# Gated-delta scans: the decayed state on ScalarE, finer convolution budgets, the attention's preparation in 27 parts and its loads in another order

## The chip, the cores and the metric

The kernel runs on one core of a Trainium2 chip. The metric is device time in microseconds (us) of one execution. Engines are named as in the profile: PE is TensorE (matmuls), PEld its weight loads, DVE VectorE, ACT ScalarE, POOL GpSimd, SP the engine that here issues the DMAs. One engine runs its instructions strictly in the order of its own queue, so an instruction that waits holds up all that stands behind it on that engine.

## The reference, cut to what matters

One layer of a hybrid backbone: 512 latent and 256 context tokens of width 2048 go through one input projection; 8 heads of a bidirectional gated delta network (GDN) and 8 heads of attention (2 key/value heads) read it; the joined result, gated by SiLU, goes through one output projection.

```python
def step(s, inp):                       # one chunk of 64 tokens of one head, one direction
    q_i, k_i, u_i, w_i, g_i, intra_i = inp
    v_new = u_i - w_i @ s
    o_i = (q_i * exp(g_i)) @ s + intra_i @ v_new
    s = s * exp(g_last) + (k_i * exp(g_last - g_i)).T @ v_new
    return s, o_i
...
qkv_g = silu(centred_conv(qkv_g, conv_w))              # 5 taps, per channel
qa, ka = apply_rope(rms_norm(qa), cos, sin), apply_rope(rms_norm(ka), cos, sin)
attn_lat = block_attention(qa, k_all, v_all) * silu(z_a)
y = concatenate([gdn_lat, attn_lat]) @ w_out
```

The line of interest is the state's: the old state `s` is scaled by one number per direction and head, and a product is added.

## The kernel before, in words

**Stages.** Modulation and the first projections fill the first 160 us of the span; eight scans, one per GDN head, run to about 860 us; the attention to about 1085; the output projection to about 1240; then a tail. Nearly every projection is made of three 512-column matmuls for each pair of 128x128 blocks (a weight is split into a high part `whi` and a low rest `wlo`). Such a weight piece takes a DMA into `wraw`, a cast to `whi` on ScalarE (L130) and a subtraction to `wlo` on VectorE (L131), with three buffers each.

**A scan.** `gdn_scan(h)` runs 12 chunk steps of head h, both directions side by side (`st` is 128x2x128). A step is a chain over three engines: PE multiplies the state by keys and queries into `ks` (L937, L939 or L942); VectorE makes `r` (L951, two halves; `rh` in the profile); PE makes `ts` from it (L956); ScalarE scales it to `vs` (L960, `vsh`); PE multiplies by `ktok` (L972); VectorE adds the decayed state `sd` and writes the new state (L978, `sth`). `sd` is the old state times its decay. It is one POOL multiply (recorded at L289, the line of the helper `mul`; `sdh` in the profile) that needs the old state, has one buffer, and is needed only by L978.

**What fills the waits of the chain.** Each of the three parts of a step yields a number of matmul columns, `F1, F2, F3 = 3900, 2700, 3200`. The driver loop pulls that many columns of projection matmuls from `feeding()` (L185) into PE's queue, so that PE works while the chain is on other engines. The parts are counted by a slot number: slot%3 = 0 stands ahead of L956, 1 ahead of L972, 2 ahead of the next `ks`. Into the same slots go the preparation of the next head (`gdn_prep(h+1)`, one part at each slot named in `PREP_AT`, with its cost in us), and the convolution jobs: the projections' results wait in a list of jobs, five taps each, the first on ScalarE and four on VectorE (L248, about 0.75 us each), then a tanh on ScalarE and products on VectorE (L286). `step_jobs` draws jobs in order while a budget is left: `CAP = (1.0, 1.6, 1.9)` by slot%3, less `spent[0]`, which holds the slot's preparation cost and 0.7 for each weight piece loaded in it.

**The last head.** Head 7 has no next head to prepare. Its slots carry `attn_prep()` instead, at the slots in `LATE_AT`: for two key/value heads and the first query head, a transpose on PE of what was stored by the projections (`kvch`, read back by DMA), squares and their sum on ScalarE (L1023), a factor by VectorE and POOL's power (L1024, L283), the product (L1026, `ktok`), the rotary table (loaded by DMA, multiplied by the norm weight; `IB` in the profile, whose room it uses), the rotation, transposes and high/low splits. V goes through the same transposes (`vtp`, L1041).

**The attention.** Units u = 0 to 16 each take one half of the queries of one head (u = 2h + qp); PE transposes the probabilities (`pt`, L1391), ScalarE and VectorE copy and split them (`pth` L1036, `ptl` L1037). ACT, DVE and POOL run in the order written there. `fill(n)` draws n pieces of three matmuls of the gate projection (`zl`, L1462), `fill(n, 2)` also two rows of the output gate (`gacc`, L1510). SP loads the merge inputs before the units: eight `o_d[i]` into `M[i]`, then `zad[i]` into `M[8+i]`, which unit u = i reads (L1567). The sixteen `M` are split into `mh` and `ml` for the output projection by `merged` (L1600).

**Before the first scan** the same `pull` lets PE run projections while the gate decays (`gates`, `gcp` L596) and the first `gdn_prep` are made.

What sets the order of instructions on an engine in the scans is a scheduler by priority, and `first_of_all()` (2500) puts `sd`, `r`, `vs` and the state update ahead of what is ready beside them; in the attention it is the written order.

Of the kernel before, what the change touches and what calls it, by code (L numbers as in the profile page):

```python
# [69 lines left out]
def build(tc, a):  # L70
# [940 lines left out]
    def rope_table(tb, i):  # L1011

        SY.dma_start(tb.rearrange("p s t d -> p (s t d)"), a["rope"])
        wv = A["nw"][:, i:i + 1]
        mul(V, tb[:, 0], tb[:, 0], wv.to_broadcast([128, 4, 128]))
        for t in range(4):
            x = tb[:, 1, t:t + 1].rearrange("p t (a s r) -> p (t a) s r", a=2, s=2)
            mul(V, x, x, swapped(wv))
        return tb

    def head_norm(ps, n, ss, jk, out):
        for t in range(n):
            S.activation(jk, ps[:, t], AF.Square, accum_out=ss[:, t:t + 1])  # L1023
        V.tensor_scalar(out=ss[:, :n], in0=ss[:, :n], scalar1=1.0 / 128.0, scalar2=EPS, op0=ALU.mult, op1=ALU.add)  # L1024
        power(ss[:, :n], -0.5)
        V.tensor_tensor(out=out, in0=ps, in1=ss[:, :n].unsqueeze(2).to_broadcast([128, n, 128]), op=ALU.mult)  # L1026

    def rope_apply(y, tb, t2):

        mul(V, t2.rearrange("p t (a s r) -> p (t a) s r", a=2, s=2), swapped(y),  # L1030
            tb[:, 1].rearrange("p t (a s r) -> p (t a) s r", a=2, s=2))
        mul(V, y, y, tb[:, 0])
        V.tensor_tensor(out=y, in0=y, in1=t2, op=ALU.add)
# [10 lines left out]
    def attn_prep():  # L1044
# [25 lines left out]
        def normed(tp, n, nm, tb, out):  # L1070
            ss = gp.tile([128, 10], F32, tag="ss", bufs=2, name=f"ss{nm}")
            NT = gp.tile([128, 6, 64], F32, tag="NT", bufs=1, name=f"NT{nm}")
            head_norm(tp, n, ss, NT[:, 0:2].rearrange("p a b -> p (a b)"), out)
            if tb is None:
                mul(V, out, out, nw[:, 1:2].to_broadcast([128, n, 128]))
                return
            t2 = gp.tile([128, 6, 128], F32, tag="vtok", bufs=2, name=f"rt2{nm}")
            rope_apply(out, tb, t2[:, :4])
# [4 lines left out]
        rope_table(tabk, 1)
        for kv in range(2):
            base = 6 * kv
            for t0, n in parts:
# [6 lines left out]
            for t0, n in parts:
                yield
                tp = transposes(chs, t0, n, bank(f"vtp{kv}{t0}")[:, :n])
                split_from(tp, vah[:, t0:t0 + n, kv * 128:kv * 128 + 128], val[:, t0:t0 + n, kv * 128:kv * 128 + 128])
# [626 lines left out]
```

## Time and profile before

| | |
|---|---|
| three runs | 1273.0, 1273.27, 1273.49 us; median 1273.27 |
| the profiled execution | 1274.02 us, its span 1271.9 us |
| TensorE clock granted in it | 0.993 of full speed on average |
| ScalarE, POOL busy | 570.1 us, 156.8 us |

The span is the time from the first to the last instruction that the profile holds; the execution's own time is 2.1 us longer. A wait for a named engine is the idle time of one engine just before an instruction, put down to what released it. A name like `sdh` stands for `sd` of any head, since numbers are left out.

### The profile page before, as it was taken

What the parts mean: (1) busy time and instruction counts of PE and PEld (TensorE: products, weight loads), DVE (VectorE), ACT (ScalarE), POOL (GpSimd) and SP (SyncE); (2) the same over time, 40 slices, a digit from 0 to 9 for tenths busy, and PEclk for the clock granted to TensorE, in tenths of its full rate; (3) what the DMA queues carried; (4) which work ended last, traced back from release to release, by engine and by line L of the source; (5) the groups of instructions that cost most, each with busy time, mean ns of one, the idle gap of its engine ahead of it and who ended that gap; (6) DMA issues with size and microseconds to landing.
All of it is one profiled execution on the core that took longest, in us unless ns stands there. A gap on an engine that the chain in (4) does not pass through costs nothing.

```text
span 1271.9 us, 24265 instructions
## 1 busy us (share of the span) xinstructions
PE 1235.5 (97%) x9242; PEld 1016.2 (80%) x9242; DVE 853.9 (67%) x1905; ACT 570.1 (45%) x1452; POOL 156.8 (12%) x206
## 2 busy tenths in 40 slices
PE   6899999999999999999999999999999999999997
PEld 4566788888888888888888887877888888787886
DVE  5444597596876778677786655547998997555433
ACT  5222373445545454454545444545555443434211
POOL 1222100111111111121211112200000000000000
PEclk9899999999999999999999999999999999999999
DMA  9999524132332223322233444357454443565202
GB/s 354 318 332 346 155 75 109 48 72 61 76 72 78 60 64 67 78 65 64 68 64 78 101 112 146 101 161 240 137 153 125 136 130 100 183 225 193 96 33 99
DMA packets 227287, 164.52 MB, mean 129 GB/s; under 512 B 62243, under 2 KB 198524, under 8 KB 226148
## 3 DMA queue, kind: packets, MB, share of 16 engines
q1 hardware_dynamic: 226874, 162.87, 44.1%
q8 instruction: 73, 1.20, 0.4%
q14 instruction: 43, 0.34, 0.1%
q10 hardware_dynamic: 297, 0.11, 0.0%
HBM read 148.85 MB, written 14.08 MB: 128 GB/s over the span
## 4 chain that ended last, share of the span: by engine, by line
PE 79%; DVE 10%; DMA 4%; ACT 3%; issue 3%; SPq 0%; POOL 0%; ACTq 0%; POOLq 0%; DVEq 0%
PE zl L1462 9%; PE kl L185 5%; PE ql L185 4%; PE vl L185 4%; PE po L148 3%; PE po L147 3%; PE po L149 3%; PE kvl L185 3%; PE tsh L972 3%; PE kx L185 2%; PE ada L404 2%; PE vx L185 2%; PE tsh L956 2%; PE klat L471 2%; PE pt L1391 2%
## 5 line engine op out<-in xcount | busy, mean ns | idle before, releaser
L960 ACT ACTIVATE vsh<-tsh,cch 128x128 f32<-128x128 f32 x88 | 32.4, 368 | 226.7 <-PE tsh L956 226.7
L289 POOL TENSOR_TENSOR sdh<-sth,egl 128x256 f32<-128x256 f32 x80 | 70.7, 884 | 445.2 <-DVE sth L978 364.3
L951 DVE SCALAR_TENSOR_TENSOR rh<-ksh,negeg,vtokh 64x128 f32<-64x128 f32 x176 | 61.2, 347 | 24.1 <-PE ksh L939 18.0
L148 PE MATMUL po<-wlo_wo,mh 128*128 128x512 f32 x192 | 76.1, 396 | 0.2 <-DVE wlo_wo L131 0.2
L147 PE MATMUL po<-whi_wo,mh 128*128 128x512 f32 x192 | 76.1, 397 | 0.0
L149 PE MATMUL po<-whi_wo,ml 128*128 128x512 f32 x192 | 76.0, 396 | 0.0
L1462 PE MATMUL zl<-hhL,whi_z 128*128 128x512 f32 x176 | 71.4, 405 | 0.0
L1462 PE MATMUL zl<-hL,whi_z 128*128 128x512 f32 x176 | 69.7, 396 | 0.0
L1462 PE MATMUL zl<-hhL,wlo_z 128*128 128x512 f32 x176 | 69.4, 395 | 0.0
L131 DVE TENSOR_TENSOR wlo_wo<-wraw_wo,whi_wo 128x512 fp32r<-128x512 f32 x48 | 33.0, 689 | 51.2 <-ACT whi_wo L130 51.1
L978 DVE TENSOR_TENSOR sth<-sdh,tsh 128x256 f32<-128x256 f32 x80 | 33.7, 421 | 44.0 <-PE tsh L972 35.7
L130 ACT CAST whi_wo<-wraw_wo 128x512 fp32r<-128x512 f32 x48 | 29.7, 618 | 57.8 <-PE po L149 47.5
L972 PE MATMUL tsh<-vsh,ktok 128*128 128x128 f32 x352 | 54.3, 277 | 0.4 <-ACT vsh L960 0.4
L972 PEld LDWEIGHTS tsh<-vsh,ktok 128*128 128x128 f32 x352 | 48.0, 191 | 3.5 <-ACT vsh L960 0.6
L1036 ACT CAST pth<-pt 128x512 fp32r<-128x512 f32 x48 | 26.5, 586 | 44.3 <-PE pt L1391 44.3
L185 PE MATMUL vl<-hhL,whi_v 128*128 128x512 f32 x112 | 46.3, 413 | 0.0
L967 ACT ACTIVATE oqh<-ksh,egsw 64x128 f32<-64x128 f32 x128 | 45.9, 358 | 0.8
L185 PE MATMUL vl<-hhL,wlo_v 128*128 128x512 f32 x112 | 46.2, 413 | 0.0
L185 PE MATMUL vl<-hL,whi_v 128*128 128x512 f32 x112 | 45.6, 408 | 0.0
L1510 DVE SCALAR_TENSOR_TENSOR gacc<-graw,scol,gacc 128x512 f32<-128x512 f32 x60 | 44.9, 748 | 1.1
L147 PEld LDWEIGHTS po<-whi_wo,mh 128*128 128x128 f32 x192 | 36.1, 188 | 9.6 <-ACT ze L1416 0.8
L148 PEld LDWEIGHTS po<-wlo_wo,mh 128*128 128x128 f32 x192 | 36.1, 188 | 9.2 <-DVE wlo_wo L131 0.6
(545 smaller groups left out, 3901.0 us busy)
## 6 DMA issues: line engine op xcount, KB each, us to landing
wada<-in_w_ada SPq DMA_DIRECT2D x64, 512.0 KB, 8.6
graw<-in_w_ada SPq DMA_DIRECT2D x64, 256.0 KB, 3.0
wraw_wo<-in_w_out SPq DMA_DIRECT2D x48, 256.0 KB, 3.0
wraw_z<-in_w_in SPq DMA_DIRECT2D x44, 256.0 KB, 3.0
wraw_v<-in_w_in SPq DMA_DIRECT2D x28, 256.0 KB, 3.1
wraw_k<-in_w_in SPq DMA_DIRECT2D x24, 256.0 KB, 2.9
wraw_q<-in_w_in SPq DMA_DIRECT2D x24, 256.0 KB, 2.8
xs<-in_x SPq DMA_DIRECT2D x4, 1024.0 KB, 8.4
```

Of the source, the lines that this page charges most:

```text
L131: (lo_eng or G).tensor_tensor(out=lo, in0=raw, in1=hi, op=ALU.subtract)
L147: T.matmul(out, lhsT=lh, rhs=rh, start=start, stop=False, skip_group_check=True)
L148: T.matmul(out, lhsT=lh, rhs=rl, start=False, stop=False, skip_group_check=True)
L149: T.matmul(out, lhsT=ll, rhs=rh, start=False, stop=stop, skip_group_check=True)
L185: T.matmul(out, lhsT=lw, rhs=rt[m], start=k == 0 and n == 0, stop=k == KT - 1 and n == 2, skip_group_check=True)
L289: eng.tensor_tensor(out=out, in0=x, in1=y, op=ALU.mult)
L951: behind["DVE"] = V.scalar_tensor_tensor(out=r[rows], in0=ks[rows, d], scalar=gsc["negeg"][rows, gcol:gcol + 1], in1=vtok[rows, p], op0=AL ...
L967: S.activation(oq[rows, v, p - 2], ks[rows, d], AF.Copy, scale=gsc["egsw"][rows, gcol:gcol + 1])
L972: T.matmul(ts[:, d], lhsT=ktok[:, p, half], rhs=vs, start=True, stop=True, skip_group_check=True)
L978: behind["DVE"] = V.tensor_tensor(out=sn, in0=sd, in1=ts[:, 0:2], op=ALU.add)
L1462: T.matmul(pl, lhsT=lw, rhs=rt, start=k == 0 and m == 0, stop=k == KT - 1 and m == 2, skip_group_check=True)
L1510: V.scalar_tensor_tensor(out=acc, in0=raw, scalar=scol[:, k:k + 1], in1=acc, op0=ALU.mult, op1=ALU.add)
```

## The change

**The decayed state.** POOL's one multiply becomes two ScalarE copies with a scale read per partition, one for each direction, at the same place in the code.

**The budgets.** A VectorE job is drawn while more than 0.2 us of budget is left, not more than 0. Five costs in `PREP_AT` rise: 1.3 to 1.6 at slots 16, 17, 19 and 20, and 0.9 to 1.1 at slot 21.

**The attention's preparation.** Its 15 parts, which stood at the odd slots 1 to 27 and at 33, are cut into 27, at slots 0, 4 to 14, 16 to 29 and 31. The helpers are cut apart: loading the rotary table, its cosine and sine products, squares, scaling, and two halves of the rotation are parts or pieces of parts of their own. The tables and `kvch` are loaded a few slots ahead of their use.

**Ahead of the scans**, one pull grows from 22000 to 25500 columns, and the first of the pulls around `gdn_prep(0)` shrinks from 5000 to 2500.

**The attention.** `M[8+i]` is loaded just before `M[i]`, for each i below NZA, so `M[8]` comes first and `M[12]` in ninth place. In the last unit `fill(3)` stands before the third `pt`. `merged(0)`, the first split for the output projection, moves from the head of the output projection into unit 12.

```diff
-        while jobs and (kind is None or kind == jobs[0][0]) and (budget > 0 if jobs[0][0] == "D" else act):
+        while jobs and (kind is None or kind == jobs[0][0]) and (budget > 0.2 if jobs[0][0] == "D" else act):
...
                         sd = gp2.tile([128, 2, 128], F32, tag="sd", bufs=1, name=f"sd{nm}_{si}")
-                        eg = egl[:, :, gcol:gcol + 1]
-                        mul(G, sd, st, (eg if dt_ == 0 else eg[:, ::-1]).to_broadcast([128, 2, 128]))
+                        for d in range(2):
+                            S.activation(sd[:, d], st[:, d], AF.Copy, scale=egl[:, d ^ dt_, gcol:gcol + 1])
...
         kn = ktoks[0].rearrange("p a s d -> p (a s) d")
+        rope_load(tabk)
         chs = load(kvd[0], "kvch00", NTOK)
-        rope_table(tabk, 1)
+        yield
+
         for kv in range(2):
...
+            tp0 = transposes(chs, 0, 2, bank(f"kps{kv}0")[:, :2])
+            r0 = squares(tp0, 2, f"k{kv}0")
+            yield
+            tp1 = transposes(chs, 2, 4, bank(f"kps{kv}2"))
+            r1 = squares(tp1, 4, f"k{kv}2")
+            chs = load(kvd[2 + kv], f"kvch{kv}1", NTOK)
+            if kv == 0:
+                yield
+                rope_cos(tabk, 1)
+                yield
+                rope_sin(tabk, 1)
+            yield
+            scaled(y0, tp0, r0)
+            mul(V, y0, y0, nw[:, 1:2].to_broadcast([128, 2, 128]))
+            yield
+            scaled(y1, tp1, r1)
+            t2 = rope_one(y1, tabk, f"k{kv}")
             if kv == 1:
-                rope_table(A["tab"], 0)
+                rope_load(A["tab"])
+            yield
+            tp = transposes(chs, 0, 2, bank(f"vtp{kv}0")[:, :2])
+            split_from(tp, vah[:, 0:2, vsl], val[:, 0:2, vsl])
+            yield
+            rope_two(y1, tabk, t2)
+            yield
...
-               18: 0, 19: 1.3, 20: 1.3, 21: 0.9, 26: 0.6, 27: 0.6, 29: 1.2, 31: 0.3, 33: 1.5}
-    LATE_AT = dict.fromkeys((*range(1, 28, 2), 33), 1.5)
+               18: 0, 19: 1.6, 20: 1.6, 21: 1.1, 26: 0.6, 27: 0.6, 29: 1.2, 31: 0.3, 33: 1.5}
+    LATE_AT = dict.fromkeys((0, *range(4, 15), *range(16, 30), 31), 1.5)
...
-    pull(22000)
+    pull(25500)
...
-    for n in (5000, 5500, 0, 0, 5500, 0, 4000, 0, 0, 14000, 0, 0, 0, 0, 0):
+    for n in (2500, 5500, 0, 0, 5500, 0, 4000, 0, 0, 14000, 0, 0, 0, 0, 0):
...
     for i in range(8):
+        if i < NZA:
+            SY.dma_start(M[8 + i], zad[i])
         SY.dma_start(M[i], o_d[i])
-    for i in range(NZA):
-        SY.dma_start(M[8 + i], zad[i])
...
+        if h >= NH:
+            fill(3)
         if before is not None:
             pts.append(attn_pt(before[0], before[1], before[2], 2))
...
+        if u == 2 * NH - 4:
+            merged(0)
...
-            if first:
+            if first and k:
                 merged(k)
```

VectorE in head 5 between the state update of step 7 and `r` of step 8 (`sth_7`, `rh_8`; `tmh` and `NEh` belong to the next head's preparation, `cacc_q` is a convolution tap, `kq` and `kc` the products at a convolution's end). Before:

```order
L832 TENSOR_TENSOR tmh_7589<-NEh_7578 96x14
L834 TENSOR_TENSOR NEh_7578<-NEh_7578,tmh_7589 96x14
L978 TENSOR_TENSOR sth_7_7832<-sdh_7_7782,tsh_7_7803 128x256
L131 TENSOR_TENSOR wlo_kv_0_7840<-wraw_kv_0_7837,whi_kv_0_7839 128x512
L248 SCALAR_TENSOR_TENSOR cacc_q_7777<-craw_1554,cvT,cacc_q_7777 128x512 x2
L951 SCALAR_TENSOR_TENSOR rh_8_7851<-ksh_7293,negeg,vtokh_6645 64x128 x2
```

After:

```order
L978 TENSOR_TENSOR sth_7_7884<-sdh_7_7836,tsh_7_7858 128x256
L131 TENSOR_TENSOR wlo_kv_0_7890<-wraw_kv_0_7887,whi_kv_0_7889 128x512
L286 SCALAR_TENSOR_TENSOR kq_7450<-craw_1553,cacc_k_7679 128x4x64
L286 SCALAR_TENSOR_TENSOR kc_7451<-craw_1553,cacc_k_7679 128x2x64
L951 SCALAR_TENSOR_TENSOR rh_8_7903<-ksh_7341,negeg,vtokh_6692 64x128 x2
```

The two taps ahead of `rh_8` have left this place, and two shorter products stand there, since taps drawn later come later in the list for all that follow.

ScalarE in head 7 between `vs` of steps 6 and 7 (`NTk` are squares of the attention's keys, `vah` a copy of V). Before:

```order
L960 ACTIVATE vsh_6_9540<-tsh_6_9538,cch_8424 128x128
L963 ACTIVATE vnh_6_9542<-tsh_6_9538,cch_8424 128x128
L967 ACTIVATE oqh_9146<-ksh_9147,egsw 64x128 x2
L1023 ACTIVATE NTk_9518,ssk_9517<-kps_9512 128x128
L1179 COPY craw_1554<-zal0a 128x512
L1023 ACTIVATE NTk_9518,ssk_9517<-kps_9512 128x128
L130 CAST whi_z1a_9554<-wraw_z1a_9552 128x512
L1023 ACTIVATE NTk_9518,ssk_9517<-kps_9512 128x128
L130 CAST whi_z1a_9589<-wraw_z1a_9587 128x512
L1036 CAST vah<-vtp_9572 128x2x128
L960 ACTIVATE vsh_7_9600<-tsh_7_9598,cch_8424 128x128
```

After:

```order
L960 ACTIVATE vsh_6_9608<-tsh_6_9606,cch_8491 128x128
L963 ACTIVATE vnh_6_9610<-tsh_6_9606,cch_8491 128x128
L967 ACTIVATE oqh_9218<-ksh_9219,egsw 64x128 x2
L1063 ACTIVATE NTk_9597,ssk_9596<-kps_9591 128x128
L130 CAST whi_z1a_9617<-wraw_z1a_9615 128x512
L1063 ACTIVATE NTk_9597,ssk_9596<-kps_9591 128x128
L130 CAST whi_z1a_9654<-wraw_z1a_9652 128x512
L949 ACTIVATE sdh_7_9646<-sth_6_9630,egl 128x128 x2
L1063 ACTIVATE NTk_9597,ssk_9596<-kps_9591 128x128
L1024 CAST vah<-vtp_9665 128x2x128
L960 ACTIVATE vsh_7_9672<-tsh_7_9670,cch_8491 128x128
```

`sd` of step 7, which reads the state of step 6, is new in the row; one square of the four now stands behind it (the first of the four stands ahead of these rows in both).

VectorE in the attention's unit 1, where `ml` of `merged(0)` stood before:

```order
L1419 SCALAR_TENSOR_TENSOR M_10031<-ze_10293,M_10031 128x512
L1441 TENSOR_TENSOR wlo_z_2_10283<-wraw_z_2_10281,whi_z_2_10282 128x512
L1037 TENSOR_TENSOR qTl_10307<-qtp_10301,qTh_10306 128x512
L1381 RECIPROCAL mx_1_10237<-mx_1_10237 128x2
L1600 TENSOR_TENSOR ml_10027<-M_10031,mh_10026 128x512
L1383 TENSOR_SCALAR pr_1_0_10249<-pr_1_0_10249,mx_1_10237 128x768
```

After, there, and then in unit 12:

```order
L1448 SCALAR_TENSOR_TENSOR M_10111<-ze_10373,M_10111 128x512
L1470 TENSOR_TENSOR wlo_z_2_10363<-wraw_z_2_10361,whi_z_2_10362 128x512
L1025 TENSOR_TENSOR qTl_10387<-qtp_10381,qTh_10386 128x512
L1410 RECIPROCAL mx_1_10317<-mx_1_10317 128x2
L1412 TENSOR_SCALAR pr_1_0_10329<-pr_1_0_10329,mx_1_10317 128x768
```

```order
L1412 TENSOR_SCALAR pr_0_0_11944<-pr_0_0_11944,mx_0_11932 128x768
L1412 TENSOR_SCALAR pr_0_1_11946<-pr_0_1_11946,mx_0_11932 128x768
L1437 COPY M_10124<-o_1_11992 128x256
L1507 TENSOR_TENSOR ml_10107<-M_10111,mh_10106 128x512
L286 SCALAR_TENSOR_TENSOR ze_12017<-ze_12017,zl_11810 128x512
L1448 SCALAR_TENSOR_TENSOR M_10118<-ze_12017,M_10118 128x512
```

`ml` no longer stands ahead of the probabilities' scaling `pr` in unit 1; in unit 12 it stands behind the scaling and ahead of a gate product.

More of the change, by code (lines that the diff above doesn't have):

```diff
@@ L1009, in swapped, with rope_load, rope_cos, rope_sin @@
         return x.rearrange("p t (a s r) -> p (t a) s r", a=2, s=2)[:, :, ::-1]
-    def rope_table(tb, i):
+    def rope_load(tb):
         SY.dma_start(tb.rearrange("p s t d -> p (s t d)"), a["rope"])
-        wv = A["nw"][:, i:i + 1]
-        mul(V, tb[:, 0], tb[:, 0], wv.to_broadcast([128, 4, 128]))
+        return tb
+    def rope_cos(tb, i):
+        mul(V, tb[:, 0], tb[:, 0], A["nw"][:, i:i + 1].to_broadcast([128, 4, 128]))
+    def rope_sin(tb, i):
         for t in range(4):
             x = tb[:, 1, t:t + 1].rearrange("p t (a s r) -> p (t a) s r", a=2, s=2)
[L1018 to L1033, printed above, removed]
+            mul(V, x, x, swapped(A["nw"][:, i:i + 1]))
     def split_from(ps_ap, hi, lo):
@@ L1068, in bank, with squares @@
             return PB.tile([128, 4, 128], F32, tag="b", name=nm)
-        def normed(tp, n, nm, tb, out):
+        def squares(tp, n, nm):
             ss = gp.tile([128, 10], F32, tag="ss", bufs=2, name=f"ss{nm}")
             NT = gp.tile([128, 6, 64], F32, tag="NT", bufs=1, name=f"NT{nm}")
[L1073 to L1078, printed above, removed]
@@ L1080, in attn_prep, with scaled @@
-        parts = ((0, 2), (2, 4))
+            jk = NT[:, 0:2].rearrange("p a b -> p (a b)")
+            for t in range(n):
+                S.activation(jk, tp[:, t], AF.Square, accum_out=ss[:, t:t + 1])
+            V.tensor_scalar(out=ss[:, :n], in0=ss[:, :n], scalar1=1.0 / 128.0, scalar2=EPS, op0=ALU.mult, op1=ALU.add)
+            power(ss[:, :n], -0.5)
+            return ss[:, :n].unsqueeze(2).to_broadcast([128, n, 128])
+        def scaled(out, tp, r):
+            V.tensor_tensor(out=out, in0=tp, in1=r, op=ALU.mult)
@@ L1081, in attn_prep, with rope_one, rope_two @@
+        def rope_one(y, tb, nm):
+            t2 = gp.tile([128, 6, 128], F32, tag="vtok", bufs=2, name=f"rt2{nm}")[:, :4]
+            mul(V, t2.rearrange("p t (a s r) -> p (t a) s r", a=2, s=2), swapped(y),
+                tb[:, 1].rearrange("p t (a s r) -> p (t a) s r", a=2, s=2))
+            return t2
+        def rope_two(y, tb, t2):
+            mul(V, y, y, tb[:, 0])
+            V.tensor_tensor(out=y, in0=y, in1=t2, op=ALU.add)
         kn = ktoks[0].rearrange("p a s d -> p (a s) d")
+        rope_load(tabk)
@@ L1082, in attn_prep @@
         chs = load(kvd[0], "kvch00", NTOK)
-        rope_table(tabk, 1)
+        yield
         for kv in range(2):
-            base = 6 * kv
-            for t0, n in parts:
-                yield
-                tp = transposes(chs, t0, n, bank(f"kps{kv}{t0}")[:, :n])
-                normed(tp, n, f"k{kv}{t0}", None if t0 == 0 else tabk, kn[:, base + t0:base + t0 + n])
-            chs = load(kvd[2 + kv], f"kvch{kv}1", NTOK)
-            if kv == 1:
-                rope_table(A["tab"], 0)
[L1093 to L1096, printed above, removed]
+            y0, y1 = [kn[:, 6 * kv + i:6 * kv + j] for i, j in ((0, 2), (2, 6))]
+            vsl = slice(kv * 128, kv * 128 + 128)
+            tp0 = transposes(chs, 0, 2, bank(f"kps{kv}0")[:, :2])
[5 more added lines that the diff above has]
+            if kv == 0:
+                yield
+                rope_cos(tabk, 1)
[7 more added lines that the diff above has]
+            t2 = rope_one(y1, tabk, f"k{kv}")
+            if kv == 1:
+                rope_load(A["tab"])
[5 more added lines that the diff above has]
+            yield
+            tp = transposes(chs, 2, 4, bank(f"vtp{kv}2"))
+            split_from(tp, vah[:, 2:6, vsl], val[:, 2:6, vsl])
@@ L1470, in fillers, with merged @@
         z_over(*over)
+    def merged(i):
+        if i >= 1:
+            mh.append(mp.tile([128, SEQ], F32R, name=f"mh{i}"))
+            ml.append(mp.tile([128, SEQ], F32R, name=f"ml{i}"))
+        S.copy(mh[i], M[i])
+        V.tensor_tensor(out=ml[i], in0=M[i], in1=mh[i], op=ALU.subtract)
     def gate_bias(acc, row):
```

29 lines of the change are left out of this document (16 added, 13 removed).

## The prediction

> **What bounds the kernel now.** I began with the page: busy time of each engine and the chain that ended last.
>
> ```profile
> PE 1235.5 (97%) x9242; PEld 1016.2 (80%) x9242; DVE 853.9 (67%) x1905; ACT 570.1 (45%) x1452; POOL 156.8 (12%) x206
> ...
> PE 79%; DVE 10%; DMA 4%; ACT 3%; issue 3%; SPq 0%; POOL 0%; ACTq 0%; POOLq 0%; DVEq 0%
> ```
>
> TensorE (PE) is busy 97 % of the span. Next I cut the span into stages, in the windows view; its columns are the stretch, its length, then busy time (instructions) of PE, PEld, DVE, ACT, POOL, then the granted clock, DMA share and GB/s. The rows are the eight scans, the attention and the output projection.
>
> ```profile
> 160.00:860.00 700.00, 692.12 (x6250) 587.47 (x6249) 495.28 (x1256) 347.46 (x993) 107.01 (x134) 1.00 0.33 83
> 860.00:1085.00 225.00, 221.66 (x1260) 186.56 (x1259) 195.66 (x320) 112.40 (x247) 9.27 (x7) 1.00 0.48 144
> 1085.00:1240.00 155.00, 154.76 (x665) 124.68 (x664) 74.68 (x120) 53.38 (x102) 0.56 (x1) 1.00 0.45 148
> ```
>
> The change adds and removes no matmul, and the clock is already 1.00, so only PE's idle time can go: 700 − 692.12 = 7.88 us in the scans and 225 − 221.66 = 3.34 us in the attention, 11.2 us together. That is the ceiling of any gain. Output projection and tail hold nothing the change can reach (155 − 154.76 = 0.24 us). Then I asked what PE waited for (who waits, for whom: us in all, times, longest), and kept the waits that lie in these two stages.
>
> ```profile
> PE tsh L956 <- DVE rh L951: 3.7, 5, 1.0
> PE pt L1391 <- DVE ptl L1037: 1.4, 2, 1.0
> PE vtp L1041 <- DMA kvch<-kvd: 1.1, 2, 0.6
> PE gcp L596 <- DVE gg__116 L589: 1.1, 1, 1.1
> PE pt L1391 <- DVE pr L1383: 0.9, 1, 0.9
> PE pxah L854 <- DVE DTh L846: 0.9, 2, 0.7
> PE pt L1391 <- ACT qn L1334: 0.8, 1, 0.8
> PE tsh L972 <- ACT vsh L960: 0.4, 1, 0.4
> ```
>
> They sum to 10.3 us: nearly all of the 11.2 sits in fifteen separate waits. So the question for each part of the change is which of them it removes, and what new ones it makes.
>
> **Part by part: the rh waits (3.7 us in five).** Here is one, in head 5 between steps 7 and 8 (timeline: start, us, engine, line, what; in brackets the idle time before it and its cause).
>
> ```profile
> 659.65 0.42 DVE L978 TENSOR_TENSOR sth<-sdh,tsh 128x256 f32<-128x256 f32 x1
> 659.99 0.69 DVE L131 TENSOR_TENSOR wlo_kv<-wraw_kv,whi_kv 128x512 fp32r<-128x512 f32 x1
> 660.15 1.00 POOL L289 TENSOR_TENSOR sdh<-sth,egl 128x256 f32<-128x256 f32 x1 [5.54 <-DVE sth L978]
> 660.59 1.89 DVE L248 SCALAR_TENSOR_TENSOR cacc_q<-craw,cvT,cacc_q 128x512 f32<-128x512 f32 x2
> 662.40 0.71 DVE L951 SCALAR_TENSOR_TENSOR rh<-ksh,negeg,vtokh 64x128 f32<-64x128 f32 x2
> 663.25 0.46 PE L956 MATMUL tsh<-rh,UU 128*128 128x128 f32 x2 [0.48 <-DVE rh L951]
> ```
>
> Between the state update (sth) and rh, VectorE does a weight piece and two convolution taps; PE runs out of projection work 0.48 us before rh is done. Three such waits are tap-made. With the stricter budget the taps go elsewhere: in the order excerpt for VectorE the two taps between sth_7 and rh_8 have become one 4x64 and one 2x64 piece of other work. Two taps cost 1.89 us here, more than twice their median:
>
> ```profile
> L248 DVE SCALAR_TENSOR_TENSOR cacc_q<-craw,cvT,cacc_q x28: 731/744/1108, 171.6 to 661.7; 128x512 f32<-128x512 f32 x28
> L289 POOL TENSOR_TENSOR sdh<-sth,egl x80: 616/997/1267, 239.1 to 824.2; 128x256 f32<-128x256 f32 x80
> ```
>
> 2 × 0.744 = 1.49, so 0.40 us is stretch beside POOL's sd (0.997 median against 0.616 at best). With sd on ScalarE this overlap is gone; 0.40 alone almost covers the 0.48. The Trainium skill, "SBUF — State Buffer", section "Who interferes with whom", says a VectorE instruction with two SBUF inputs and a GpSimd instruction that reads SBUF share a port pair, and the one that starts first blocks the other. The trace agrees in direction (1.89 against 1.49). By that rule VectorE would get back up to 80 × 0.62, about 50 us (an estimate), of queue time in the scans; moved taps would then cost nothing, and the sum below would be −7.7 instead of −7.1.
>
> The other two of the five lie in head 7 and are not tap-made.
>
> ```profile
> 767.44 0.89 DVE L289 TENSOR_TENSOR IB<-IB,nw 128x512 f32<-128x512 f32 x2 [1.42 <-DMA IB<-in_rope]
> ...
> 769.11 0.46 PE L956 MATMUL tsh<-rh,UU 128*128 128x128 f32 x2 [1.02 <-DVE rh L951]
> ```
>
> ```profile
> 823.71 0.42 DVE L978 TENSOR_TENSOR sth<-sdh,tsh 128x256 f32<-128x256 f32 x1 [2.20 <-PE tsh L972]
> ...
> 825.90 1.01 POOL L283 TENSOR_TENSOR ssq<-ssq,expo 128x4 f32<-128x4 f32 x1 [0.69 <-DVE ssq L1024]
> ...
> 826.94 0.69 DVE L1026 TENSOR_TENSOR ktok<-qps,ssq 128x512 f32<-128x512 f32 x1 [1.12 <-POOL ssq L283]
> 827.55 0.70 DVE L951 SCALAR_TENSOR_TENSOR rh<-ksh,negeg,vtokh 64x128 f32<-64x128 f32 x2
> ...
> 828.40 0.46 PE L956 MATMUL tsh<-rh,UU 128*128 128x128 f32 x2 [0.89 <-DVE rh L951]
> ```
>
> In the first, VectorE stands 1.42 us in front of the rope table's load, with rh queued behind it. In the second it stands 1.12 us for POOL's power, again ahead of rh. The 27 parts load the table several slots before its product, and put the squares a slot or more ahead of the scaling. So 1.02 and 0.89 go, and the three tap waits are 3.7 − 1.02 − 0.89 = 1.8. Removed: 1.8 + 1.02 + 0.89 = 3.7 us.
>
> **The other removed waits.** The earlier kvch load takes the two vtp waits (1.1): several slots lie between load and transpose now, not one; behind the earlier loads SP's queue holds only weight pieces, which three buffers cover. The gcp wait (1.1) is before the first scan, where 3500 more columns are pulled, seven 512-column matmuls. At 154.76/665 = 0.233 us each that is 1.6 us of cover: it goes. Those columns are missing later (2500 of them from the next pull), where I see no wait. Of pxah's 0.9 I take 0.5, between 0 (taps land there) and 0.9. In the attention:
>
> ```profile
> 869.43 0.63 ACT L1567 ACTIVATE zae<-M 128x512 f32<-128x512 f32 x1 [2.88 <-DMA M<-zad]
> 870.59 0.66 PE L1391 MATMUL pt<-cmain,pr 128*128 128x128 f32 x4 [0.83 <-ACT qn L1334]
> 883.55 0.69 DVE L1600 TENSOR_TENSOR ml<-M,mh 128x512 fp32r<-128x512 f32 x1
> 884.92 1.31 PE L1391 MATMUL pt<-cmain,pr 128*128 128x128 f32 x8 [0.94 <-DVE pr L1383]
> 1070.38 0.65 PE L1391 MATMUL pt<-cmain,pr 128*128 128x128 f32 x4 [1.02 <-DVE ptl L1037]
> ```
>
> ScalarE stands 2.88 us for M[8], which was ninth in the load order; now it is first, and the 0.8 behind it goes. M[12] moves up too, but only to ninth place, and its tile is read four units later. At 883.55 ml (0.69) sits directly ahead of pr; it leaves for unit 12 (order excerpt), so of the 0.94 I take 0.7. At 1070.38 fill(3) puts three pieces of three matmuls, 9 × 0.233 = 2.1 us, ahead of the pt that waited 1.02: gone; I count 1.2 of that group's 1.4.
>
> Removed in all: 3.7 + 1.1 + 1.1 + 0.5 + 0.8 + 0.7 + 1.2 = 9.1 us. The 0.4 before L972 stays.
>
> **What is added.** The two copies on ScalarE have no row before. Nearest are same-size ScalarE instructions with a per-partition scale:
>
> ```profile
> 694.62 1.28 ACT L995 ACTIVATE oqh<-oqh,msh 128x128 f32<-128x128 f32 x4 [1.45 <-POOL msh L283]
> 695.81 0.35 ACT L960 ACTIVATE vsh<-tsh,cch 128x128 f32<-128x128 f32 x1
> ```
>
> Four overlapped take 1.28, 0.32 apiece, and one alone takes 0.35, so a pair lies between 2 × 0.32 = 0.64 and 2 × 0.35 = 0.70; I take 0.68. That is 80 × 0.68 = 54 us more on an engine with 700 − 347 = 353 us free in the scans. Behind each sd, which waits for sth, stand on ScalarE weight casts, craw takes (which free a PSUM bank) and the next vsh. The waits view shows ScalarE's slack there:
>
> ```profile
> ACT vsh L960 <- PE tsh L956: 226.7, 78, 7.0
> ```
>
> 226.7/78 = 2.9 us idle on average before vsh, four times 0.68. Four terms:
>
> (a) Head 7, step 7. In ScalarE's order excerpt the fourth square (0.28, row below) is now behind sd_7, hence behind sth_6; on its result hang POOL's power, the ktok scaling and then rh_7.
>
> ```profile
> L1023 ACT ACTIVATE NTk<-kps x12: 277/278/293, 771.4 to 804.9; 128x128 f32<-128x128 f32 x12
> ```
>
> Chain from the end of sth: 0.68 + 0.28 + 1.01 + 0.69 = 2.66, with some 0.3 of handing over 3.0. Taking the 823.71 rows as the pattern: sth ends at 824.13, and rh would have had to start 0.89 earlier, at 826.66, for PE not to wait, which allows 2.53. So +0.5 (0 to 0.9, the wait of that pattern).
>
> (b) ml at unit 12 is 0.69 ahead of that unit's merge, where VectorE idles little:
>
> ```profile
> 1031.30 0.17 DVE L1337 TENSOR_SCALAR hss<-hss 128x4 f32<-128x4 f32 x1 [0.30 <-ACT hjk L1336]
> ```
>
> 0.69 − 0.30 = 0.4 is the worst for a waiting PE; I take +0.3 (0 to 0.4).
>
> (c) Where a head begins, ScalarE has no idle left: the 695.81 vsh starts right behind the four L995. sd should fall into the 1.45 us that L995 waits for POOL, yet some may not: seven heads × 0.68 = 4.8 at most. I take +0.6, near the lower end because 1.45 is twice 0.68.
>
> (d) Taps not drawn now are drawn later, toward a head's end: 0 to 1.8 (the waits they made before), taken +0.6, since POOL's stretch is off them.
>
> Sum: −9.1 + 0.5 + 0.3 + 0.6 + 0.6 = −7.1 us. The profiled execution took 1274.02, 0.75 above the median of the runs (1273.27) and 2.1 over its own span: 1274.02 − 7.1 = 1266.9, and for the median 1273.27 − 7.1 = 1266.2 us.
>
> **Rivals.** *Everything goes and nothing new appears*: all 10.3 us, 1263.0. For it: ScalarE's 2.9 us of slack. Against: (a), which the order fixes.
>
> *The taps' waits return elsewhere*: 1.8 and pxah's 0.5 stay lost and (d) is at its bound 1.8, so −6.8 + 0.5 + 0.3 + 0.6 + 1.8 = −3.6, 1269.7. For it: VectorE's work is the same amount, 495 of 700 us. Against: less stretch.
>
> *The change does not do what it says*: each wait is replaced by one nearby, because PE ran dry for lack of filling columns there and the number of columns is unchanged; within 2.5 us, about 1272.5. For it: the columns are the same in sum. Against: five of the waits have a named cause that leaves.
>
> *Slower, by ScalarE's in-order queue*: sd waits at the head of ScalarE's queue for sth, and casts, craw takes and vsh come late behind it. The place is L972's wait for vsh. If each of 80 steps loses 0.15 us, (c) is 12.0 instead of 0.6: −7.1 + 11.4 = +4.3, 1277.6. It decides once (c) passes 10.2, that is 15 steps at the full 0.68. Against it: only one such wait, 0.4, exists now. For it: the mean of 2.9 hides steps with none.
>
> **How the numbers follow.** A measurement here can tell about 0.2 %, 2.5 us, from no change. Forecast (−5 to −9): 0.56. Everything goes: 0.12. Taps return: 0.14. No effect: 0.12. Slower: 0.06. So faster 0.82, same 0.12, slower 0.06. The range's low end is the ceiling, 11.2 us off: 1262.1. Its high end is the taps rival with (a) at 0.9, (b) at 0.4 and (c) at 1.3, so −2.4: 1270.9.
>
> **What would show it.** The profile after should have no POOL sd; 160 ScalarE copies of about 0.35; taps near 0.744; no PE wait for rh above 0.5 except at head 7, step 7; no kvch, gcp or qn wait; scans idle some 4 us and attention 1 us instead of 7.9 and 3.3. It is wrong if L972's wait for vsh grows past 2 us, if rh waits still sum to 3, or if PE's own busy time changes by more than 1 us.

## The result and the profile after

The changed kernel takes 1266.99 us (median of 6 runs, 1266.65 to 1267.89), the kernel before 1273.38 in the same comparison (1273.0 to 1275.35). The ratio is 0.9948, with a 95 % interval of 0.9935 to 0.9961: 6.6 us faster (5.0 to 8.3). The profiled execution's span fell from 1271.9 to 1264.9 us. Forecast were 7.1 us and 1266.2.

The sum was right; its terms were not. To see that, the span is cut at two events that both programs have, not at fixed times: the first `ts` of head 0 and the first `ts` of head 7. The windows view of before (stretch, length, then busy time and instructions of PE, PEld, DVE, ACT, POOL, the clock, DMA share, GB/s):

```profile
0.00:235.72 235.72, 217.58 (x1615) 158.48 (x1616) 133.68 (x353) 87.80 (x189) 41.04 (x66) 0.97 0.75 232
235.72:762.16 526.44, 522.92 (x5066) 446.92 (x5065) 389.35 (x986) 264.40 (x766) 89.55 (x111) 1.00 0.30 72
762.16:1271.90 509.74, 494.99 (x2563) 410.77 (x2561) 330.92 (x568) 217.87 (x497) 26.25 (x29) 1.00 0.46 141
```

The same of the changed kernel:

```profile
0.00:235.74 235.74, 214.07 (x1617) 155.97 (x1618) 133.06 (x353) 87.89 (x189) 41.06 (x66) 0.98 0.75 232
235.74:761.76 526.02, 521.12 (x5066) 446.93 (x5065) 374.34 (x986) 305.56 (x906) 25.51 (x41) 1.00 0.30 72
761.76:1264.90 503.14, 493.85 (x2561) 411.02 (x2559) 329.98 (x568) 224.43 (x517) 18.83 (x19) 0.99 0.47 143
```

Up to head 0 the length is the same. Its inside is not: PE waited longer for the modulation's weights, which the change does not touch, so what the pulls are worth cannot be read from this stretch (before, then changed):

```profile
PE ada L404 <- DMA wada<-in_w_ada: 2.6, 3, 1.8
```

```profile
PE ada L404 <- DMA wada<-in_w_ada: 6.0, 4, 2.6
```

Heads 0 to 6, where the new `sd` and the budgets work, gained 0.4 us with the same 5066 matmuls. All the rest, 6.6 us, came from head 7 and the attention. The forecast had −1.1, −1.1 and −4.9 for the three. VectorE's busy time in heads 0 to 6 fell by 15.0 us (389.35 to 374.34) and bought next to nothing. Where that went is what the experiments ask.

What PE waits for in the scans of the changed kernel (us in all, times, longest):

```profile
PE tsh L956 <- DVE rh L951: 1.6, 3, 0.9
PE t1h L708 <- DVE kq L286: 1.6, 1, 1.6
PE qal2a L185 <- ACT whi_q2a L130: 1.5, 1, 1.5
PE tsh L972 <- ACT vsh L960: 0.8, 2, 0.6
PE ksh L942 <- DVE sth L978: 0.6, 1, 0.6
PE tsh L956 <- DVE UU L904: 0.6, 2, 0.3
PE qal2a L185 <- DVE wlo_q2a L131: 0.4, 1, 0.4
PE kvl L185 <- DVE wlo_kv L131: 0.3, 1, 0.3
```

The waits for kvch, gcp and pxah are gone, and those for r fell from 3.7 to 1.6. But others are new or longer, above all a product of the first preparation (t1h), a weight cast (qal2a), vs, and late UU blocks.

The place of the prediction's first timeline, head 5 between steps 7 and 8, did become what was forecast. VectorE:

```profile
656.96 0.42 DVE L978 TENSOR_TENSOR sth<-sdh,tsh 128x256 f32<-128x256 f32 x1
657.37 0.69 DVE L131 TENSOR_TENSOR wlo_kv<-wraw_kv,whi_kv 128x512 fp32r<-128x512 f32 x1
657.98 0.42 DVE L286 SCALAR_TENSOR_TENSOR kq<-craw,cacc_k 128x256 f32<-128x256 f32 x1
658.32 0.28 DVE L286 SCALAR_TENSOR_TENSOR kc<-craw,cacc_k 128x128 f32<-128x128 f32 x1
658.96 0.71 DVE L951 SCALAR_TENSOR_TENSOR rh<-ksh,negeg,vtokh 64x128 f32<-64x128 f32 x2 [0.36 <-PE ksh L939]
```

Now r waits for PE, not PE for r. In the attention no wait of PE is named any more, and in the fixed stretch that holds most of it PE idles 0.25 us:

```profile
860.00:1085.00 225.00, 224.75 (x1271) 188.78 (x1270) 198.52 (x326) 117.49 (x257) 9.27 (x7) 1.00 0.48 143
```

And term (a), head 7 before step 7, is there as the order had it: ScalarE's copies of `sd` first, behind them the fourth square, then VectorE, POOL's power, the scaling, r.

```profile
802.27 0.69 ACT L949 ACTIVATE sdh<-sth,egl 128x128 f32<-128x128 f32 x2
...
802.86 0.26 ACT L1063 ACTIVATE NTk<-kps 128x128 f32<-128x128 f32 x1
...
803.24 0.17 DVE L1064 TENSOR_SCALAR ssk<-ssk 128x4 f32<-128x4 f32 x1 [0.94 <-ACT NTk L1063]
...
803.56 1.01 POOL L283 TENSOR_TENSOR ssk<-ssk,expo 128x4 f32<-128x4 f32 x1 [4.90 <-DVE ssk L1064]
...
804.60 0.69 DVE L1069 TENSOR_TENSOR ktok<-kps,ssk 128x512 f32<-128x512 f32 x1 [1.19 <-POOL ssk L283]
...
805.21 0.70 DVE L951 SCALAR_TENSOR_TENSOR rh<-ksh,negeg,vtokh 64x128 f32<-64x128 f32 x2
...
806.06 0.46 PE L956 MATMUL tsh<-rh,UU 128*128 128x128 f32 x2 [0.89 <-DVE rh L951]
```

The pair of copies took 0.69 us (0.68 was reckoned), and the wait 0.89 where 0.5 was taken (0 to 0.9). The chain was longer than reckoned: the state update ends at 801.55 and `rh` starts at 805.21, 3.66 us later and not 3.0. The copies start 0.72 us behind the update, since a weight cast (L130, 0.61 us from 801.75) stands ahead of them on ScalarE; the sum had left it out.

### The profile page after: what moved, and what is told of

Its sections match the earlier page's. It is cut to its first block, busy times and chain, and to the rows that moved or that the text cites. A ratio compares the mean times of both kernels' runs of the same rounds, so it can differ in the third digit from the quotient of the medians.

```text
span 1264.9 us, 24327 instructions
## 1 busy us (share of the span) xinstructions
PE 1229.0 (97%) x9242; PEld 1013.9 (80%) x9242; DVE 837.4 (66%) x1905; ACT 617.9 (49%) x1612; POOL 85.4 (7%) x126
## 4 chain that ended last, share of the span: by engine, by line
PE 75%; DVE 3%; ACT 3%; issue 1%; POOL 1%; ACTq 0%; POOLq 0%; DVEq 0%
PE zl L1491 10%; PE vl L185 6%; PE ql L185 5%; PE po L147 4%; PE po L148 4%; PE po L149 4%; PE kl L185 4%; PE vx L185 3%; PE tsh L972 3%; PE kx L185 2%; PE tsh L956 2%; PE pt L1420 2%; PE kvl L185 1%; DVE cacc_v L248 1%; PE ksh L937 1%
## 5 line engine op out<-in xcount | busy, mean ns | idle before, releaser
L949 ACT ACTIVATE sdh<-sth,egl 128x128 f32<-128x128 f32 x160 | 55.5, 396 | 18.5 <-DVE sth L978 17.7
L130 ACT CAST whi_wo<-wraw_wo 128x512 fp32r<-128x512 f32 x48 | 29.6, 619 | 60.7 <-PE po L149 52.6
L972 PE MATMUL tsh<-vsh,ktok 128*128 128x128 f32 x352 | 54.6, 278 | 0.9 <-ACT vsh L960 0.8
L972 PEld LDWEIGHTS tsh<-vsh,ktok 128*128 128x128 f32 x352 | 48.3, 191 | 5.0 <-ACT vsh L960 1.6
```

The lines of the kernel that those rows point to most:

```text
L949: S.activation(sd[:, d], st[:, d], AF.Copy, scale=egl[:, d ^ dt_, gcol:gcol + 1])
L972: T.matmul(ts[:, d], lhsT=ktok[:, p, half], rhs=vs, start=True, stop=True, skip_group_check=True)
```

## The experiments

Theory: the gain is a sum of separate waits. Rivals: the ScalarE copies carry it, or they only cost; the budgets carry it, or do nothing. All results in one table: the median, its ratio to the kernel before on the same chip, and the three stretches of the profiled execution cut as above (span up to head 0, heads 0 to 6, head 7 to the end). A stretch is from one execution, a median from 4 to 11.

| | median us | ratio (95 %) | to head 0 | heads 0–6 | from head 7 |
|---|---|---|---|---|---|
| before | 1273.38 | 1 | 235.7 | 526.4 | 509.7 |
| changed | 1266.99 | 0.9948 (0.9935–0.9961) | 235.7 | 526.0 | 503.1 |
| 1 copies alone | 1267.72 | 0.9954 (0.9942–0.9966) | 237.6 | 523.1 | 507.6 |
| 2 changed, copies undone | 1265.38 | 0.9934 (0.9922–0.9947) | 236.6 | 524.6 | 503.8 |
| 3 changed, budgets undone | 1263.44 | 0.9917 (0.9904–0.9931) | 235.3 | 522.9 | 503.1 |
| 4 parts and attention alone | 1268.3 | 0.9954 (0.9941–0.9968) | 235.0 | 526.9 | 503.1 |
| 5 as 1, POOL kept busy | 1274.64 | 1.0008 (0.9999–1.0017) | 238.5 | 528.2 | 507.3 |
| 6 as 1, copies twice | 1269.2 | 0.9968 (0.9956–0.9981) | 236.3 | 523.3 | 508.0 |
| 7 changed, threshold undone | 1264.35 | 0.9928 (0.9916–0.9941) | 235.6 | 522.7 | 503.1 |
| 8 as 3, first pull 5000 | 1262.71 | 0.9917 (0.9903–0.993) | 236.5 | 521.6 | 502.5 |
| 9 threshold alone | 1269.29 | 0.9963 (0.995–0.9977) | 239.0 | 522.5 | 507.6 |
| 10 copies and threshold | 1269.31 | 0.9966 (0.9954–0.9979) | 236.7 | 523.0 | 508.2 |
| 11 as 8, parts a slot earlier | 1261.49 | 0.9905 (0.9892–0.9919) | 236.7 | 521.6 | 501.2 |
| 12 copies and whole budgets | 1270.01 | 0.9978 (0.9969–0.9987) | 234.3 | 524.2 | 508.7 |

The stretch up to head 0 differs by up to 4.7 us between programs that are alike there (9 and 12), so single terms are read from the two other columns. In heads 0 to 6 two pairs of programs that are alike there agree better: 526.4 and 526.9 (before and 4), 521.6 and 521.6 (8 and 11). From head 7 on the noise is larger. Seven programs have the old attention, and from its first `pt` to the end they take 401.2 to 402.7 us, the kernel before the longest of them; six of the seven with the new one take 399.6 to 399.7, experiment 2 takes 401.0.

**1, the copies alone.**

```diff
 (kernel before)
-                        eg = egl[:, :, gcol:gcol + 1]
-                        mul(G, sd, st, ...)
+                        for d in range(2):
+                            S.activation(sd[:, d], st[:, d], AF.Copy, scale=egl[:, d ^ dt_, gcol:gcol + 1])
```

> The kernel before with one edit: the decayed state made by two ScalarE copies; budgets, parts and attention as before. Sum of separate waits (the theory): VectorE's tap stretch goes, which takes 1 to 1.8 us of the waits for r away, and ScalarE's queue adds 0.6 to 2.4 us of new ones: within 1 us of the kernel before. Rival, the ScalarE copies carry the gain (VectorE gets 16.5 us of busy time back): 3 us or more faster. Rival, the copies only cost (in the changed kernel a cast 1.5 us late, vs 0.8, a square 0.9): 2 to 3 us slower.

5.9 us faster by the ratio, 3.4 us of it in heads 0 to 6 and 2.1 from head 7 on: the rival that gives the copies the gain is what came, and my theory (within 1 us) fell.

**2, the copies undone in the changed kernel** (the same lines, the other way).

> The changed kernel with one edit undone: the decayed state again one POOL multiply. Sum of separate waits: 1267 within 1 us, the wait for the cast (1.5 us) and that behind the fourth square (0.9) gone, two tap waits of 0.5 to 0.8 back. Rival, the copies carry the gain: 1270 or more. Rival, the copies only cost: 1265 or less.

1265.38, no slower than the changed kernel (between my theory and the rival that the copies only cost): 524.6 in heads 0 to 6 against 526.0. So in heads 0 to 6 the copies are worth 3.4 us alone and −1.5 us beside the rest of the change. The terms are not separate. Term (a) shows here too: without the copies the wait for `r` at step 7 of head 7 is 0.22 us and not 0.89.

```profile
804.79 0.46 PE L956 MATMUL tsh<-rh,UU 128*128 128x128 f32 x2 [0.22 <-DVE rh L951]
```

**3, the budgets undone in the changed kernel.**

```diff
-... (budget > 0.2 if jobs[0][0] == "D" else act):
+... (budget > 0 if jobs[0][0] == "D" else act):
...
-16: 1.6, 17: 1.6, 18: 0, 19: 1.6, 20: 1.6, 21: 1.1
+16: 1.3, 17: 1.3, 18: 0, 19: 1.3, 20: 1.3, 21: 0.9
```

> The changed kernel with the budgets undone: a job drawn while more than 0 is left, the five costs as before. Sum of separate waits: three tap waits come back, shorter since POOL no longer stretches taps, 0.5 to 1.5 us in all: 1267.5 to 1268.5. Rival, the finer budgets carry the scans' part: 1269 or more. Rival, with the sd off POOL they do nothing: 1267 within 0.4.

Below all three: 1263.44, 3.1 us less in heads 0 to 6. The budgets cost, beside the copies.

**4, the 27 parts and the attention's edits on the kernel before.**

> The kernel before with the 27 parts of the attention's preparation and the attention's three edits (load order, the filling before the last transposes, the early split); sd on POOL, budgets and pulls as before. Sum of separate waits: head 7 loses 1.0 + 0.9 + 1.1 us of waits, the attention 3.1: 6.1 us faster, 1267.3. Rival, the copies or the budgets carry half of it: not over 4 us faster, 1269.4 or more.

Head 7 to the end takes 503.1, as in the changed kernel, and heads 0 to 6 are as before: this part is separate, and carries nearly all of the measured gain (5.9 of 6.6 us by the ratio). The 27 parts and the attention's three edits went in together; which wait each took away is read from the waits that are gone, not from runs of their own.

**5, POOL kept busy.** The copies as in 1, and POOL's old multiply beside them, into a tile that nothing reads:

```diff
 (kernel of 1)
+                        sx = gp2.tile([128, 2, 128], F32, tag="sx", bufs=1, name=f"sx{nm}_{si}")
+                        eg = egl[:, :, gcol:gcol + 1]
+                        mul(G, sx, st, (eg if dt_ == 0 else eg[:, ::-1]).to_broadcast([128, 2, 128]))
```

> The kernel of the first experiment (decayed state on ScalarE, all else as before) with POOL's old multiply kept beside it, into a tile that nothing reads; VectorE's order is the same instruction for instruction. Theory, sharing between POOL and VectorE: VectorE's busy time returns from 837.6 to about 853, the waits for r from 2.2 to about 3.7 us, heads 0 to 6 from 523.0 to about 526 us: 3 to 5 us slower than the first experiment. Rival, the gain lies in when the decayed state is ready or in POOL's freed queue for other work: within 0.7 us of the first experiment.

This is the cleanest pair of the study. Heads 0 to 6 of 1, then of 5:

```profile
237.55:760.60 523.05, 520.96 (x5066) 447.32 (x5065) 373.75 (x986) 306.84 (x906) 26.35 (x41) 1.00 0.31 72
```

```profile
238.52:766.76 528.24, 524.37 (x5066) 447.13 (x5065) 388.98 (x986) 307.15 (x906) 86.77 (x111) 1.00 0.30 72
```

The same 986 VectorE instructions take 15.2 us longer, and the stretch 5.2 us longer, for POOL work that nobody waits for. One kind of tap shows it (duration ns min/median/max), of 1, then of 5:

```profile
L248 DVE SCALAR_TENSOR_TENSOR cacc_q<-craw,cvT,cacc_q x28: 730/744/753, 172.8 to 660.4; 128x512 f32<-128x512 f32 x28
```

```profile
L248 DVE SCALAR_TENSOR_TENSOR cacc_q<-craw,cvT,cacc_q x28: 729/746/1107, 173.7 to 666.7; 128x512 f32<-128x512 f32 x28
```

The median stays; among the taps that meet POOL are some of up to 1107, where 753 was the most. So the gain of the copies in heads 0 to 6 is that VectorE's instructions are no longer stretched. (The waits that the view names for r rose only from 2.2 to 2.7 us; why that understates it comes below.) The stretch is also 1.8 us longer than in the kernel before: the copies by themselves cost something, which the relief of VectorE more than pays for in experiment 1.

**6, the copies twice,** the second pair into a tile that nothing reads (two more lines like those of 1).

> The kernel of the first experiment with a second pair of the same two ScalarE copies, into a tile that nothing reads: 55 us more on ScalarE. Theory, ScalarE has slack without the finer budgets: 0 to 1.5 us slower than the first experiment. Rival, each pair costs at the head of ScalarE's queue: 3 us or more slower (0.04 us or more for each of 80 steps), waits for vs and for casts above 3 us together.

```profile
236.32:759.61 523.29, 520.72 (x5066) 446.97 (x5065) 374.43 (x986) 346.30 (x1046) 26.73 (x41) 1.00 0.31 72
```

40 us more on ScalarE, 0.2 us more time: without the new budgets ScalarE has room. The medians differ by 1.5 us, at the edge of what was expected, but not in this stretch. The prediction's rival of a slower kernel, by ScalarE's queue, falls for the copies by themselves.

**7, the threshold alone undone** in the changed kernel, the raised costs kept.

> The changed kernel with the threshold alone undone (a job drawn while more than 0 is left), the five raised costs kept. All of the budgets undone gave about 3.5 us. Theory, the threshold moves taps to where ScalarE is now full, so it carries the loss: 2 us or more faster than the changed kernel. Rival, the raised costs carry it: within 1 us of the changed kernel.

522.7 in heads 0 to 6, against 526.0: the threshold carries the whole loss, as long as the costs are raised.

**8, the budgets undone and the first pull back at 5000.**

> The changed kernel with the budgets undone and the first pull around the first preparation back at 5000 columns (25500 kept). Theory, the smaller pull made the new wait of 1.6 us for kq (t1h): it goes, 1.0 to 1.6 us faster than with the budgets undone alone. Rival, the 2500 columns are missed where they come from: within 0.5 us of it.

The ratio is the same as in 3, so nothing is gained that can be told. The t1h wait shrank to 0.6, and in its place PE waited for another weight piece:

```profile
PE kvl L185 <- DVE wlo_kv L131: 1.2, 1, 1.2
PE tsh L972 <- ACT vsh L960: 1.0, 3, 0.4
PE tsh L956 <- DVE rh L951: 0.9, 1, 0.9
PE t1h L708 <- DVE kq L286: 0.6, 1, 0.6
```

**9 and 10, the threshold alone, and with the copies,** on the kernel before.

```diff
-... (budget > 0 if jobs[0][0] == "D" else act):
+... (budget > 0.2 if jobs[0][0] == "D" else act):
```

> The kernel before with the stricter threshold alone (a job drawn while more than 0.2 is left); the decayed state stays on POOL. Theory, the threshold and the ScalarE copies both remove the waits that taps make behind POOL's stretch: alone it helps, 0.5 to 2 us faster than the kernel before. Rival, the threshold costs by itself, whatever engine makes the decayed state: 2 us or more slower.

> The kernel before with the ScalarE copies and the stricter threshold together, nothing else. Theory, the taps pile up where a head ends and the next begins, where ScalarE is full with the copies: 2 to 3.5 us slower than the copies alone, about 1270 to 1271. Rival, both gains add: 1 us or more faster than the copies alone. Rival, what made the threshold dear in the changed kernel was the raised costs beside it or the 27 parts: within 0.7 us of the copies alone.

Heads 0 to 6 take 526.4 with neither, 523.1 with the copies, 522.5 with the threshold, 523.0 with both. Each alone takes 3.4 to 4.0 us, and together they take no more. Both cure the same ill, taps in the way of r; what the two together save there beyond one of them goes again in longer waits for vs, as the table in the next section shows. Experiment 9 is 4.7 us faster by the ratio, more than the 2 at most that I expected. My expectation for 10 (2 to 3.5 us slower than 1) fell by the stretch; by the ratio 10 is 1.5 us slower than 1, with intervals that overlap.

**11, the preparation's parts from slot 16 on one slot earlier.**

```diff
 (kernel of 8)
-    LATE_AT = dict.fromkeys((0, *range(4, 15), *range(16, 30), 31), 1.5)
+    LATE_AT = dict.fromkeys((0, *range(4, 29), 31), 1.5)
```

> The changed kernel with the budgets undone, the first pull back at 5000, and the attention's preparation from slot 16 on one slot earlier (slots 0, 4 to 28, 31): in ScalarE's order all squares of the second key/value head then stand ahead of the copies of step 7. Theory, the wait for r of 0.9 us in head 7 came of the square behind the copies: it goes, 0.5 to 0.9 us faster than without the shift (1262.7 there). Rival, it comes of the transposes' place: as before within 0.3 us. Rival, the shifted parts meet another step: slower by 0.5 us or more.

The wait of 0.9 for r is gone; from head 7 on 501.2 instead of 502.5, and the median 1.2 us lower. This version has the lowest ratio of all, 0.9905, though its interval overlaps with those of 3 and 8. It does not show that the copies made the wait. In experiment 8, from which it differs by the shift alone, all four squares already stand ahead of the copies of step 7 (the last starts at 798.81, the copies at 799.08), and the wait is there all the same, with a product of the rotation ahead of `rh`:

```profile
801.29 0.69 DVE L289 TENSOR_TENSOR rt2k<-ktok,IB 128x512 f32<-128x512 f32 x1
801.90 0.71 DVE L951 SCALAR_TENSOR_TENSOR rh<-ksh,negeg,vtokh 64x128 f32<-64x128 f32 x2
...
802.76 0.46 PE L956 MATMUL tsh<-rh,UU 128*128 128x128 f32 x2 [0.90 <-DVE rh L951]
```

The shift takes the whole chain of power, scaling and rotation away from this step, and so cures both. That the copies push it is shown by experiment 2.

**12, the copies with the whole budgets,** threshold and costs, on the kernel before.

> The kernel before with the ScalarE copies and the whole of the budgets (threshold and the five raised costs), nothing else. In VectorE's order 35 taps now stand between the last r of a head and the first r of the next (before 10, with the copies and the threshold alone 24, in the changed kernel 37). Theory, threshold and raised costs together push taps over the head's end, and that costs: heads 0 to 6 take 525.5 us or more (523.0 with the copies and the threshold alone), about 1271 to 1272.5 in all. Rival, the loss needs the pulls' other phase or the 27 parts: within 0.7 us of the copies and the threshold alone.

524.2: between theory (525.5 or more) and rival (within 0.7 of 523.0). In heads 0 to 6 the budgets as a whole cost 1.1 us here, 3.1 in the changed kernel. By the ratios, 0.9978 against 0.9954 for experiment 1, they cost 3.1 us here too; another 1.1 of that stands from head 7 on, where the noise is as large.

## Why the prediction came out right, step by step

**The removed waits of head 7 and the attention** (−4.9 net) held. Experiment 4 shows them alone: 6.6 us. The named waits of this stretch sum to 6.1 us before, and 0.9 came back as (a), which leaves 5.2: (b) made no wait (0.3 forecast), the `pt` waits behind VectorE went wholly, not 1.9 of 2.3, and (a) cost 0.9, not 0.5. The other 1.4 us stand behind no named wait. About one of them can be this single execution, since the kernel before is the longest of the seven programs with its attention; the rest stays open.

**The tap waits** (−1.8): the mechanism was right, the size too small. I took it from the waits that the view names. But PE's busy time hides more: with the same 5066 matmuls, heads 0 to 6 were PE-busy for 522.92 us before and 520.96 in experiment 1. Matmul ends are modelled, and a matmul that starts late can still count as busy. The start times show it. Take each matmul's distance from the start of the one before it, less the lower quartile for the same pair of lines and shapes, and add up what is over 0.05 us. By this measure PE lost 7.5 us ahead of `ts` in 51 places of heads 0 to 6 before, more than all of its idle time there (526.44 − 522.92 = 3.5). In us, with the sum over all matmuls, most of which is the same in every program:

| heads 0 to 6 | ahead of `ts` (L956) | ahead of L972 (vs) | ahead of qal2a | all | stretch |
|---|---|---|---|---|---|
| before | 7.5 | 1.3 | 0.8 | 42.3 | 526.4 |
| 1 copies alone | 3.9 | 1.9 | 0.8 | 39.0 | 523.1 |
| 5 as 1, POOL kept busy | 7.5 | 2.2 | 0.8 | 43.5 | 528.2 |
| 9 threshold alone | 4.8 | 1.3 | 0.8 | 38.3 | 522.5 |
| 10 copies and threshold | 2.8 | 3.5 | 0.8 | 38.6 | 523.0 |
| 12 copies and whole budgets | 4.0 | 3.8 | 0.8 | 39.8 | 524.2 |
| changed | 5.0 | 2.5 | 3.2 | 42.1 | 526.0 |
| 7 changed, threshold undone | 3.7 | 2.7 | 0.9 | 38.5 | 522.7 |
| 2 changed, copies undone | 6.5 | 1.6 | 1.9 | 40.4 | 524.6 |

The copies halve what is lost ahead of `ts`, and POOL's multiply brings it all back: the stretch of VectorE does reach PE through `r`. In the changed kernel 2.5 us of the 7.5 went, but L972 and qal2a took 3.6 back.

**The signs that I named.** Two of them spoke against the prediction. I had called it wrong if PE's own busy time changed by more than 1 us. The page of the changed kernel has 1229.0 where 1235.5 stood:

```profile
PE 1229.0 (97%) x9242; PEld 1013.9 (80%) x9242; DVE 837.4 (66%) x1905; ACT 617.9 (49%) x1612; POOL 85.4 (7%) x126
```

Of these 6.5 us, 3.5 lie ahead of head 0, 1.8 in heads 0 to 6 and 1.1 behind. So busy time can fall with no matmul less, and the idle time of 11.2 us was no ceiling by its nature. Whether a gain beat it is not shown: experiment 11 is 12.1 us faster, with an interval of 10.3 to 13.8. And the scans, from 160 to 860 us, were to idle some 4 us: they idle 7.75 (7.88 before), since new waits took the place of the old ones.

**The Trainium skill's rule** ("SBUF — State Buffer", "Who interferes with whom"), which I used for one alternative only, is what experiments 1 and 5 show at work: a VectorE instruction with two inputs in SBUF stretches when POOL reads SBUF beside it. In direction the traces agree: whichever of the two starts second is the longer for it (numbers in the last section). The size is another: VectorE got back 15.0 us in heads 0 to 6, not the estimated 50. The estimate had laid all of POOL's time on VectorE. But part of the loss was POOL's own: its 70 multiplies in heads 0 to 6 of experiment 5 took 60.4 us, 17.4 more than 70 times the shortest (0.614).

**Term (d), taps that come later** (+0.6, at most 1.8), is the step that failed. The threshold's effect in the changed kernel is 526.0 − 522.7 = +3.3. Of the 128 taps (L248) of these heads, those that start between the last `ts` of a head and the second of the next number 6 before, 12 in experiment 7, 18 in experiment 10, 32 in experiment 12 and 36 in the changed kernel. Where heads meet, ScalarE's one queue also holds the old head's squares and four scalings and the casts of the coming weights. There the largest new wait arose, between heads 5 and 6 (ScalarE, then PE):

```profile
692.84 1.28 ACT L995 ACTIVATE oqh<-oqh,msh 128x128 f32<-128x128 f32 x4 [1.25 <-POOL msh L283]
694.02 0.35 ACT L960 ACTIVATE vsh<-tsh,cch 128x128 f32<-128x128 f32 x1
694.27 0.26 ACT L711 ACTIVATE NTh<-t1h 128x128 f32<-128x128 f32 x1
...
694.52 1.13 ACT L130 CAST whi_q2a<-wraw_q2a 128x512 fp32r<-128x512 f32 x2
```

```profile
695.18 0.50 PE L185 MATMUL qal2a<-hhL,whi_q2a 128*128 128x512 f32 x1 [1.47 <-ACT whi_q2a L130]
```

The casts stand behind the L995 that wait for POOL's power: the place that term (c) named, with a cast late, not a vs. With the threshold undone only one cast for qal2a stands behind the L995 there, not two. So (c) and (d) together were +1.2 in the sum, and the threshold alone measured +3.3. The table above says where it went: against experiment 7, 2.3 us ahead of qal2a and 1.3 ahead of `ts`. The place is where heads meet: all ten losses over 0.3 us of the changed kernel lie between 5 us ahead of a head's first `ts` and 12 us behind it, while four of the five largest before lay 50 to 60 us into a head. In experiments 1, 10 and 12 the losses over 0.2 us ahead of L972 all lie 8 to 9 us behind a head's first `ts`, so term (c) had its place right too; they grew from 1 to 10 as the taps there went from 6 to 18.

That the number of taps alone is to blame is not shown. In experiment 12, with nearly as many taps there but the old pulls and parts, the budgets cost 1.1 us, and qal2a lost nothing more; in experiment 2, with 35 and POOL's `sd`, heads 0 to 6 were 1.5 us shorter than in the changed kernel. The loss ahead of qal2a comes only where the budgets meet the new pulls and parts (1.9 in experiment 2, 3.2 in the changed kernel). The parts come in head 7 alone, behind this stretch, so the pulls' other phase is the likelier reason; no run tried either.

**gcp** (−1.1): the wait went, and t1h's 1.6 came, right where 2500 columns had been taken away and I saw no wait. Not all of it is theirs: with the old pulls t1h waits 0.7 to 1.0 us in experiments 1, 4, 9 and 12. With the columns back (experiment 8) it is 0.6, but kvl waits 0.9 longer. What the larger pull is worth stays open: up to head 0 the two kernels take 235.72 and 235.74 us, with 3.4 us more of waits for the modulation's weights in the second, and no run undid it alone.

So a right total came of errors that cancelled, and that is luck: the end of VectorE's stretch and head 7 gave more than forecast, the taps' new place and t1h took it back.

## What to carry to other kernels

Work on an idle engine is not free: here 60 us of POOL multiplies, which no one waited for, cost 5 us by stretching VectorE. Two edits that cure the same wait need not add, and the second can cost: test each on the version that has the other, and undo parts of a change that won. Waits that a profile names are a lower bound of what a chain loses where matmul ends are modelled (here 1.8 us named ahead of `ts` in heads 0 to 6, and 7.5 lost); compare the length of a stretch with equal instruction counts instead.
